# Splitting the final norm by token halves and moving late weight splits in a one-core streaming-encoder kernel

## Chip, cores and metric

The kernel runs on one NeuronCore of a Trainium2 chip. The metric is the device time of one execution in microseconds (us), lower is better; the time of before is the median of three runs. A profile gives every engine's instructions of one such execution, with times from the start of its span. The engines are TensorE (PE, matrix products; PEld is its weight load), VectorE (DVE), ScalarE (ACT), GpSimd (POOL), and SyncE (SP), which only issues transfers here.

## What is computed

One step of a one-layer encoder, for 512 prompt tokens and 32 sample tokens (544 together). A norm and a wide input projection feed two recurrent branches (an mLSTM with four heads, and HGRN2), which are merged by gates. The change lies in what follows the merge, at the end of the layer:

```python
y = jax.nn.sigmoid(ga) * ya + jax.nn.sigmoid(gb) * yb
h = h + y @ w_out[l]
h = h + jax.nn.sigmoid(h @ w_pg[l]) * (p[l] @ w_ple[l])
...
out = _rmsnorm(h, final_g)
```

`w_out` and `w_pg` are 1024 x 1024, `w_ple` is 256 x 1024. The mLSTM also returns its matrix memory C per head (512 x 512, with the normaliser as a further column), a product of all its keys and values; for the last head that product is computed at the very end of the kernel, between the steps of the final norm.

## The kernel before

**Layout.** Activations are kept transposed: 1024 channels as eight tiles of 128 partitions, with the 544 tokens as columns. A token half is 272 columns (`one`, `other`; `TH` = 272). float32 accuracy comes from splitting each operand into a high and a low part of a shorter format and adding three products (high x high, high x low, low x high). The high part is a cast on ScalarE (L132 for weights), the low part a subtraction (L133), on VectorE unless `eng` says otherwise.

**The wide products** `y @ w_out` and `h @ w_pg` use a two-by-two scheme with seven block products in place of eight. Class `Two` does this for a pair of output tiles, k and k+4: its weight blocks are a11, a12, a22 and sums s1 to s4, its moving operands are halves of the activation (`h1s`) or sums of those halves (`hf`, made by `half_sums`, L1995 to L2010, called by `h_sums`). Each block is twelve products of 128 x 272 on TensorE, accumulated in two PSUM tiles `d`, one for each token half. The methods `after1` to `after7` copy a partial sum to SBUF (`keep`, ScalarE, L609) or combine one with a PSUM tile into the output (`put`, VectorE L616 and L618, or ScalarE L620). An output tile pair has four quarters: tile 0 or 1, token half 0 or 1. `Pump` orders the blocks of four pairs, loads their weights three blocks ahead, and splits them. Trace names carry unit numbers: `wa11104` is block a11 of the first gate pair, `ws2107` is block s2 of the last. Split weights live in five rotating buffers, so a cast waits until TensorE has read the block five splits before it.

**Around the change**, in program order:

- the four pairs of `w_out`, whose `out` (L2057) adds the residual, splits the new h into high and low (L2062, L2063), and calls `h_sums` for the last pair (L2065);
- `ple_units(3, ...)` (L1979), the last three of eight embedding products `p @ w_ple` (names wple5 to wple7; twelve products of 128 x 272 each), their PSUM tiles copied out by L1987;
- the four pairs of `w_pg`. `gate_out` (L2089) applies the sigmoid, multiplies by the embedding product (L2093), adds to h (L2094), squares (L2095) and adds the square to a running sum `total` (L2097);
- the C memory of the last head (`memories`): three blocks of 24 products (L1041) and one of 2 x 12 (L1064), written out by ScalarE's queue. After five steps of six products `rms_cols` (L225 on) sums `total` over channels with tiny products into `r1pc` (L233) and takes the reciprocal root on VectorE with three Newton rounds (`rsqrt`, L183 to L185); after four more steps `norm_bcast` spreads the root over partitions with products `r1pb` (L248), and `norm_out` scales eight tiles of h (VectorE L2135, GpSimd L2132) and sends each as one transfer of y (SP, L2136).

**Order.** TensorE's order is the program's order (`manual_schedule`). The order on the other engines is set by the framework's scheduler when the program is built, from the data dependences and from marks such as `high_priority` and `issue_after`. Each engine works through its own list in order; an instruction that waits holds up all behind it.

Of the kernel before, what the change touches and what calls it, by code (L numbers as in the profile page):

```python
# [59 lines left out]
TAIL = (5, 4)  # L60
# [7 lines left out]
def hybrid_step(ctx: ExitStack, tc: tile.TileContext, a, o):  # L68
# [408 lines left out]
    class Two:  # L477
# [4 lines left out]
        def __init__(self, outs, early=False, apart=False, src=None, made_=None):  # L482
# [3 lines left out]
            self.hook = None  # L486
# [125 lines left out]
        def put(self, i, b, ps, t, how):  # L612
            with tc.high_priority(FIRST) if self.urgent else tc.high_priority():
                for d, c in self.tiles[i][1][b]:
# [4 lines left out]
                    else:  # L619
                        S.mul(d, ps[:, c], -1.0)  # L620

# [1435 lines left out]
    def out(f, t):  # L2057
# [6 lines left out]
        if f % HK == HK - 1 and h1[HK - 1] is not None and h1[KD - 1] is not None:  # L2064
            h_sums(HK - 1)  # L2065
# [20 lines left out]
    tokens = [(0, NS)] + [(NS + b * P, P) for b in range(NB)]  # L2086
    total = []

    def gate_out(f, t):  # L2089

        for c in (one, other) if f % HK == HK - 1 else (slice(0, T),):
            S.activation(t[:, c], t[:, c], AF.Sigmoid)
            V.tensor_tensor(t[:, c], t[:, c], ple[f][:, c], ALU.mult)  # L2093
            V.tensor_tensor(h1[f][:, c], h1[f][:, c], t[:, c], ALU.add)  # L2094
            S.activation(t[:, c], h1[f][:, c], AF.Square)  # L2095
            if total:
                V.tensor_tensor(total[0][:, c], total[0][:, c], t[:, c], ALU.add)  # L2097
        if not total:
# [8 lines left out]
            ("w_pg", k),  # L2107
        )
# [16 lines left out]
    def norm_out(pb):  # L2125
        rows = slot("rows")
        S.copy(rows[:, NS:T], pb[:, 0, :])
        S.copy(rows[:, :NS], pb[:, 1, :NS])  # L2128
        for f in (0, 4, 1, 2, 5, 3, 7, 6):
            t = h1[f]  # L2130
            if f in aside:
                G.tensor_tensor(t[:, :T], t[:, :T], rows[:, :T], ALU.mult)  # L2132
            else:
                for d, c in ((t[:, NS:T], pb[:, 0, :]), (t[:, :NS], pb[:, 1, :NS])):
# [125 lines left out]
```

## Time and profile before

| what | us |
|---|---|
| median of three runs | 1110.12 (1109.43 to 1111.32) |
| the profiled execution's own time | 1109.81 |
| its span in the profile | 1108.1 |
| TensorE busy with products | 1093.3 |
| VectorE busy | 924.2 |
| ScalarE busy | 693.0 |
| GpSimd busy | 206.2 |

Rows of the timeline read: start, duration (both us), engine, line, operation, output <- input, shape, and in square brackets how long the engine stood idle before it and what ended that. "x2" is two instructions merged into a row. Rows of one engine can overlap a little, since an instruction's start and its predecessor's end are pipelined. In a list of waits a row gives who waited for whom, the total, how often, and the longest.

### The profile page before, as it was taken

Reading aid. Unit: us, or ns where it says so; the run is one execution under the profiler, and the core shown is the slowest. Engines: PE = TensorE matmul, PEld = TensorE weight load, DVE = VectorE, ACT = ScalarE, POOL = GpSimd, SP = SyncE. Lnnn points to the kernel's source line nnn. Section 1 sums busy time; section 2 is a strip of 40 time slices with the busy share of each in tenths; the row PEclk is TensorE's granted clock in tenths of the full one; section 3 lists DMA queues with packets and bytes.
Section 4 is the critical chain, followed back from the end, with each engine's and each line's share of the span. In section 5 each row is a group of like instructions: output and inputs, shape, how many; then the busy total and the mean of one; then the engine's idle time right before and its main releaser. Section 6 shows DMA issues by size and latency. Waiting matters only on the chain. (4 is left out here: it accounts for less than half of the span.)

```text
span 1108.1 us, 23728 instructions
## 1 busy us (share of the span) xinstructions
PE 1093.3 (99%) x8621; PEld 1071.8 (97%) x8621; DVE 924.2 (83%) x2088; ACT 693.0 (63%) x1578; POOL 206.2 (19%) x370
## 2 busy tenths in 40 slices
PE   9999999999999999999999999999999999999897
PEld 9899999999999999999999999999999999999897
DVE  7889988686896786976888799999999977778785
ACT  6767557754666555665665477777676667446573
POOL 7204010303022031202220132232222210000001
PEclk9999999999999999999999999999999999999999
DMA  6135315639355286543898665666666682336843
GB/s 231 58 118 191 126 58 178 157 130 219 118 178 189 86 180 178 159 166 136 219 260 253 176 141 143 144 140 138 157 153 145 160 218 86 115 122 216 279 131 120
DMA packets 96398, 176.58 MB, mean 159 GB/s; under 512 B 11156, under 2 KB 16788, under 8 KB 96024
## 3 DMA queue, kind: packets, MB, share of 16 engines
q1 hardware_dynamic: 80352, 141.43, 39.9%
q0 software_dynamic: 15040, 32.51, 16.0%
q8 instruction: 68, 1.11, 0.4%
q10 hardware_dynamic: 888, 1.12, 0.3%
q14 instruction: 50, 0.41, 0.1%
HBM read 150.10 MB, written 41.69 MB: 173 GB/s over the span
## 5 line engine op out<-in xcount | busy, mean ns | idle before, releaser
L495 POOL DMA_DIRECT2D ws<-in_w_in x46 | 39.7, 862 | 211.0 <-DVE hkq L1818 35.6
L609 ACT COPY t<-d 128x272 f32<-128x272 f32 x153 | 58.1, 380 | 10.8 <-PE d L595 10.8
L1818 DVE TENSOR_TENSOR hkq<-hkq,q 128x288 f32<-128x288 f32 (+1 forms) x96 | 40.8, 432 | 2.8 <-PE pl L1800 1.1
L749 DVE SCALAR_TENSOR_TENSOR cv<-ub,vec,cv 128x547 f32<-128x547 f32 x48 | 37.6, 784 | 1.6 <-ACT cv L744 1.2
L2132 POOL TENSOR_TENSOR h<-h,rows 128x544 f32<-128x544 f32 x3 | 4.0, 1359 | 184.8 <-ACT rows L2128 184.8
L1800 PE MATMUL pl<-hkq,km 128*128 128x128 f32 x224 | 36.3, 283 | 1.0 <-ACT km L1786 1.0
L1786 ACT COPY km<-hkq 128x256 f32<-128x256 f32 x56 | 24.0, 428 | 14.6 <-DVE hkq L1818 5.9
L1800 PEld LDWEIGHTS pl<-hkq,km 128*128 128x128 f32 x224 | 30.3, 189 | 2.4 <-ACT km L1786 1.9
L1155 DVE SCALAR_TENSOR_TENSOR c<-c,wi,Cs 128x258 f32<-128x258 f32 x32 | 15.3, 479 | 18.6 <-PE Cs L1153 18.4
L1318 DVE TENSOR_TENSOR y<-ya,y 128x272 f32<-128x272 f32 x48 | 18.9, 435 | 12.0 <-PE ya L167 10.2
L1053 ACT COPY Co<-C 128x258 f32<-128x258 f32 x30 | 9.8, 378 | 29.6 <-PE C L1041 27.2
L1825 DVE COPY_PREDICATED at<-lmask,pl 128x256 f32<-128x256 uint8 (+1 forms) x56 | 25.3, 452 | 0.1
L741 POOL COPY uo<-ub 128x3 f32<-128x3 f32 x16 | 18.7, 1166 | 34.5 <-DVE ub L618 26.6
L1232 ACT COPY y<-nm 128x516 f32<-128x516 f32 x16 | 9.5, 591 | 22.9 <-PE nm L1221 22.4
L925 POOL COPY vsm<-vt 128x96 f32<-128x96 f32 x12 | 6.2, 517 | 86.1 <-ACT vt L620 43.8
L925 POOL COPY ksm<-kf 128x96 f32<-128x96 f32 x16 | 6.3, 399 | 84.3 <-ACT kf L939 84.3
L1765 POOL TENSOR_SCALAR_AFFINE_SELECT aa<-at 128x128 f32<-128x128 f32 x32 | 19.6, 643 | 8.2 <-DVE at L1825 8.0
L1209 DVE BATCH_NORM_STATS2 bs<-y 128x6 f32<-128x512 f32 (+1 forms) x20 | 13.8, 692 | 8.2 <-ACT y L1232 8.0
L570 POOL DMA_DIRECT2D ws<-in_w_in x14 | 14.1, 1007 | 32.3 <-DVE ws272l L133 26.8
L1221 PE MATMUL nm<-vhl,sh 128*128 128x258 f32 x112 | 18.4, 286 | 0.0
L376 POOL DMA_DIRECT2D w_pg_d<-in_w_pg x16 | 13.1, 816 | 24.0 <-issue 23.1
L1924 ACT ACTIVATE osq<-kq 128x128 f32<-128x128 f32 x32 | 9.8, 305 | 12.4 <-DVE kq L1919 12.1
(4733 smaller groups left out, 5083.8 us busy)
## 6 DMA issues: line engine op xcount, KB each, us to landing
ws<-in_w_in POOLq DMA_DIRECT2D x60, 256.0 KB, 4.8
ws<-in_w_in SPq DMA_DIRECT2D x46, 256.0 KB, 3.7
ya_d<-y SPq DMA_DIRECT2D x32, 272.0 KB, 2.5
y<-ya_d SPq DMA_DIRECT2D x24, 272.0 KB, 3.5
w_out_d<-in_w_out POOLq DMA_DIRECT2D x24, 256.0 KB, 6.0
w_pg_d<-in_w_pg POOLq DMA_DIRECT2D x24, 256.0 KB, 6.3
c<-in_C SPq DMA_DIRECT2D x16, 258.0 KB, 3.8
out_Cs<-c SPq DMA_DIRECT2D x16, 258.0 KB, 3.9
```

The lines of the kernel that those rows point to most:

```text
L495: G.dma_start(t, piece(u, i), accum_op=ALU.add)
L609: self.kept = S.copy(t, ps)
L741: G.tensor_copy(uo[:, ft, 0, :], ub[:, 547:550])
L749: V.scalar_tensor_tensor(cv[:, :547], ub[:, j : j + 547], vcol(V_CW + 4 * ft + j), cv[:, :547], ALU.mult, ALU.add)
L1155: V.scalar_tensor_tensor(c0[f][:, v], c0[f][:, v], wi[:, NS - 1 : NS], pn[:, :VH], ALU.mult, ALU.add)
L1221: PE.matmul(pn[:, g, :VH], st[j][x][:, (i - j) * P : (i - j + 1) * P], vv[j][y][:, g * VH : (g + 1) * VH], start=(j == 0 and q == 0), stop ...
L1318: add = V.tensor_tensor(y[:, half(b)], acc[b], y[:, half(b)], ALU.add)
L1765: G.affine_select(out=out, in_=x, compare_op=ALU.is_gt, fill=0.0, base=0, pattern=[[-sign, n]], channel_multiplier=sign)
L1786: low = S.copy(km.rearrange("p (n j c) -> p n j c", j=2, c=c), view(kk, HB, ((2 * c, NA // (2 * c)), (c - HB, 2), (1, c))),)
L1800: PE.matmul(out, km[:, b * P : (b + 1) * P], view(qq, b * P, dims), start=True, stop=True)
L1818: V.tensor_tensor(x, x, d, ALU.mult)
L1825: V.copy_predicated(at[:, :n], lmask[:, li, :n], pn[:, 0, :n])
```

## The change

It has three parts.

1. The low splits of wple5 to wple7 go from VectorE to GpSimd, and the sums of h for the last pair are made after the first two gate weights are split, not in `out`.
2. The last gate pair gets its own block order (`parts`): a11, a12, s2, a22, s3, s1, s4. It uses four PSUM tiles, and `gate_out` runs for each quarter as it is complete: tile 0 and tile 1 of the first token half, then tile 1 and tile 0 of the second.
3. The final norm runs for each token half by itself: column sums, root, broadcast, scaling, and eight transfers of y of 128 x 272 for each half. The first half's column sums stand after one step of C, the second half's after five, followed at once by the first half's broadcast; the second half's broadcast comes four steps later.

```diff
-TAIL = (5, 4)
+TAIL = (4, 4)
...
         def blocks(self, times):
+            if self.parts:
+                m, (s2, s1, s3, a22, s4) = self.made, sorted(times[2:])
+                return [
+                    (times[0], [(a, 0)], self.make("a11"), self.run("a11", 0, True, self.after1), []),
+                    (times[1], [(a, 1)], self.make("a12"), self.run("a12", 1, True, self.first), []),
+                    (s2, [(m, 1)], self.make("s2"), self.run("s2", 0, False, self.after6), []),
+                    (s1, [(b, 1)], self.make("a22"), self.run("a22", 2, True, self.second), []),
+                    (s3, [(m, 2)], self.make("s3"), self.run("s3", 0, False, self.third), []),
+                    (a22, [(m, 0)], self.make("s1"), self.run("s1", 1, True, self.fourth), [k[1]]),
+                    (s4, [(m, 3)], self.make("s4"), self.run("s4", 3, True, self.fifth), [k[0]]),
+                ]
...
+                if half == 2:
+                    self.ps = self.ps + phalves(f"d{self.other}")
...
+        def done(self, i, b, ps, t, how):
+            self.put(i, b, ps, t, how)
+            self.parts(i, b, self.tiles[i][0])
+
+        def first(self, ps):
+            self.done(0, 0, ps, self.t["t1"], "add")
+
+        def second(self, ps):
+            self.keep("t4", ps)
+
+        def third(self, ps):
+            self.keep("t167", ps)
+            self.done(1, 0, ps, self.t["t4"], "minus")
+
+        def fourth(self, ps):
+            t = self.t["t16"]
+            with tc.high_priority():
+                V.tensor_tensor(t, t, ps, ALU.add)
+            self.done(1, 1, ps, self.t["t167"], "minus")
+
+        def fifth(self, ps):
+            self.done(0, 1, ps, self.t["t16"], "add")
...
-                w = weight(a["w_ple"][f], f"wple{f}", cols=2 * P)
+                w = weight(a["w_ple"][f], f"wple{f}", cols=2 * P, eng=V if f < 5 else G)
...
-        if f % HK == HK - 1 and h1[HK - 1] is not None and h1[KD - 1] is not None:
-            h_sums(HK - 1)
...
-    tokens = [(0, NS)] + [(NS + b * P, P) for b in range(NB)]
+    blocks = ((0, P), (P, P), (2 * P, TH - 2 * P))
...
-    def gate_out(f, t):
+    def gate_out(f, t, c=slice(0, T)):
...
+            (lambda i, b, t: gate_out(HK - 1 + i * HK, t, half(b))) if k == HK - 1 else None,
...
-    def norm_bcast(r):
-        pb = paux("r1pb")
-        for b in range(NB):
-            bcast(pb[:, 0, b * P : (b + 1) * P], r, b + 1, P)
-        bcast(pb[:, 1, :NS], r, 0, NS)
+    def norm_bcast(b, r):
+        pb = paux(f"r1pb{b}")
+        for i, (t0, m) in enumerate(blocks):
+            bcast(pb[:, 0, t0 : t0 + m], r, i, m)
         return pb
...
-    def norm_out(pb):
-        rows = slot("rows")
-        S.copy(rows[:, NS:T], pb[:, 0, :])
-        S.copy(rows[:, :NS], pb[:, 1, :NS])
+    def norm_out(b, pb):
+        rows = slot(f"rows{b}")
+        S.copy(rows[:, :TH], pb[:, 0, :TH])
         for f in (0, 4, 1, 2, 5, 3, 7, 6):
-            t = h1[f]
+            t = h1[f][:, half(b)]
             if f in aside:
-                G.tensor_tensor(t[:, :T], t[:, :T], rows[:, :T], ALU.mult)
+                G.tensor_tensor(t, t, rows[:, :TH], ALU.mult)
             else:
-                for d, c in ((t[:, NS:T], pb[:, 0, :]), (t[:, :NS], pb[:, 1, :NS])):
-                    V.scalar_tensor_tensor(d, d, vcol(V_FG + f), c, ALU.mult, ALU.mult)
-            nc.sync.dma_start(o["y"][f], t[:, :T])
+                V.scalar_tensor_tensor(t, t, vcol(V_FG + f), pb[:, 0, :TH], ALU.mult, ALU.mult)
+            nc.sync.dma_start(o["y"][f, :, half(b)], t)
...
         pump = Pump(gates_)
+        pump.prepare(2)
+        h_sums(HK - 1)
         pump.to(2)
...
         rest = memories()
+        next(rest)
+        r = rms_cols(total[0][:, one], blocks, "r10")
+        norm_scale()
         for _ in range(TAIL[0]):
             next(rest)
-        r = rms_cols(total[0], tokens, "r1")
-        norm_scale()
+        r1 = rms_cols(total[0][:, other], blocks, "r11")
+        norm_out(0, norm_bcast(0, r))
         for _ in range(TAIL[1]):
             next(rest)
-        norm_out(norm_bcast(r))
+        norm_out(1, norm_bcast(1, r1))
```

VectorE's list at the head of the gate product, before: `h3u`, `h3v`, `hfl`, `hfx` are the sums of h for the last pair and their low parts, the names with `l` behind a number are low splits of weights.

```order
L2058 TENSOR_TENSOR h_14848<-h_14848,res_14846 128x544
L1998 TENSOR_TENSOR h3u<-h_14845 128x272
L1999 TENSOR_TENSOR h3u<-h_14848,h_14845 128x272
L2000 TENSOR_TENSOR h3v_15029<-h3u,h_14848 128x272
L2063 TENSOR_TENSOR h_15005<-h_14845,h_15005 128x272
L2001 TENSOR_TENSOR h3v_15030<-h3v_15029,h_14848 128x272
L2063 TENSOR_TENSOR h_15022<-h_14848,h_15022 128x544
L2007 TENSOR_TENSOR hfl_15026<-h3u,hfh_15025 128x544
L2008 TENSOR_TENSOR h_15005<-h3v_15030,h_15005 128x272
L2009 SCALAR_TENSOR_TENSOR hfx_15027<-h3v_15029,hfx_15027 128x272
L133 TENSOR_TENSOR wple60l<-wple6r_15064,wple60h 128x256
L133 TENSOR_TENSOR wple70l<-wple7r_15087,wple70h 128x256
```

The same place on VectorE now, from the low part of the new h on:

```order
L2099 TENSOR_TENSOR h_15005<-h_14845,h_15005 128x272
L133 TENSOR_TENSOR wa11104l<-wi104r_15097,wa11104h 128x512
L133 TENSOR_TENSOR wa12104l<-wi104r_15099,wa12104h 128x512
L2099 TENSOR_TENSOR h_15022<-h_14848,h_15022 128x544
L2034 TENSOR_TENSOR h3u<-h_14845 128x272
L2035 TENSOR_TENSOR h3u<-h_14848,h_14845 128x272
L2036 TENSOR_TENSOR h3v_15121<-h3u,h_14848 128x272
L133 TENSOR_TENSOR ws2104l<-ww_pg0r_15101,ws2104h 128x512
L2037 TENSOR_TENSOR h3v_15122<-h3v_15121,h_14848 128x272
L133 TENSOR_TENSOR ws1104l<-ww_pg0r_15103,ws1104h 128x512
L2044 TENSOR_TENSOR h_15005<-h3v_15122,h_15005 128x272
L2043 TENSOR_TENSOR hfl_15118<-h3u,hfh_15117 128x544
```

The embedding splits have left VectorE's list, and four weight splits that stood behind the sums now stand among or ahead of them; `hfx` of the last pair is the next row behind those shown. GpSimd's list gains three rows ahead of the norm's:

```order
L133 TENSOR_TENSOR wple50l<-wple5r_15025,wple50h 128x256
L133 TENSOR_TENSOR wple60l<-wple6r_15048,wple60h 128x256
L133 TENSOR_TENSOR wple70l<-wple7r_15071,wple70h 128x256
L2164 TENSOR_TENSOR h_14404<-h_14404,rows_15832 128x272
L2164 TENSOR_TENSOR h_14510<-h_14510,rows_15832 128x272
```

Before, GpSimd's list had nothing between its last transfers and the norm's three products. The third place is the end of VectorE's list. Before, the running sum `pg_15148` is finished, then one chain of the root follows:

```order
L2094 TENSOR_TENSOR h_14848<-h_14848,pg_15565 128x272
L2097 TENSOR_TENSOR pg_15148<-pg_15148,pg_15565 128x272 x2
L240 TENSOR_SCALAR rms_s<-r1pc 32x1
L240 TENSOR_SCALAR rms_s<-r1pc 128x4
L180 TENSOR_SCALAR rsq_t<-rms_s 128x5
L181 TENSOR_SCALAR rms_r<-rsq_t 128x5
```

Now two chains run into each other; this piece is the end of the first half's root (`r10pc`) and the beginning of the second's (`r11pc`):

```order
L185 SCALAR_TENSOR_TENSOR rms_r<-rsq_u,rms_r 128x3
L240 TENSOR_SCALAR rms_s<-r11pc 128x2
L183 TENSOR_TENSOR rsq_u<-rms_r 128x3
L240 TENSOR_SCALAR rms_s<-r11pc 16x1
L184 SCALAR_TENSOR_TENSOR rsq_u<-rsq_u,rms_s 128x3
L180 TENSOR_SCALAR rsq_t<-rms_s 128x3
L185 SCALAR_TENSOR_TENSOR rms_r<-rsq_u,rms_r 128x3
L181 TENSOR_SCALAR rms_r<-rsq_t 128x3
```

The last Newton round of the first half (L183, L184, and the second L185 row) now stands behind the reading of `r11pc`, which TensorE makes four steps of C later than `r10pc`; likewise the reading of `r10pc` stands ahead of the last quarter's addition to h.

More of the change, by code (lines that the diff above doesn't have):

```diff
@@ L2085, in hybrid_step @@
     kw, vv = xs[:NB], xs[NB:]
-    tokens = [(0, NS)] + [(NS + b * P, P) for b in range(NB)]
+    blocks = ((0, P), (P, P), (2 * P, TH - 2 * P))
     total = []
-    def gate_out(f, t):
[L2091 to L2098, printed above, removed]
+    def gate_out(f, t, c=slice(0, T)):
+        S.activation(t[:, c], t[:, c], AF.Sigmoid)
+        V.tensor_tensor(t[:, c], t[:, c], ple[f][:, c], ALU.mult)
+        V.tensor_tensor(h1[f][:, c], h1[f][:, c], t[:, c], ALU.add)
+        S.activation(t[:, c], h1[f][:, c], AF.Square)
+        if total:
+            V.tensor_tensor(total[0][:, c], total[0][:, c], t[:, c], ALU.add)
+        else:
             total.append(t)
```

4 lines of the change are left out of this document (2 added, 2 removed).

## Prediction

> **What bounds the kernel now.** I start with the page, then ask who made TensorE wait, since that engine is busy 99% of the span.
>
> ```profile
> span 1108.1 us, 23728 instructions
> PE 1093.3 (99%) x8621; PEld 1071.8 (97%) x8621; DVE 924.2 (83%) x2088; ACT 693.0 (63%) x1578; POOL 206.2 (19%) x370
> ```
>
> The view of TensorE's waits over the whole span has one long entry (the next is 1.1 us), and it lies just where the change works:
>
> ```profile
> PE ple L167 <- DVE wple60l L133: 4.2, 1, 4.2
> ```
>
> The chain of waits that ended last shows what it holds up, and that everything behind it is TensorE's own work up to the last eviction:
>
> ```profile
> 1040.00 0.35 DVE wple60l L133
> ...
> 1040.39 4.30 PE ple L167 x20
> 1044.69 42.08 PE d L595 x336
> 1086.77 3.63 PE C L1041 x30
> 1090.40 1.14 PE r1pc L233 x10
> 1091.54 2.99 PE C L1041 x24
> 1094.53 1.22 PE r1pb L248 x10
> ...
> 1101.02 0.37 ACT Co L1071
> ```
>
> So a microsecond taken from TensorE before 1086 is a microsecond of the span. Behind 1101.4 only transfers are left; they are the second bound, weighed below.
>
> **The embedding products and the last sums of h.** TensorE's rows around the wait, two products to a row, and then four stage windows (width, then busy time of TensorE, its weight loads, VectorE, ScalarE and GpSimd, granted clock, DMA share, GB/s):
>
> ```profile
> 1034.05 0.41 PE L167 MATMUL ple<-ps0h,wple50h 128*128 128x272 f32 x2
> 1035.56 0.41 PE L167 MATMUL ple<-ps0h,wple60h 128*128 128x272 f32 x2
> 1040.39 0.56 PE L167 MATMUL ple<-ps0h,wple60l 128*128 128x272 f32 x2 [4.18 <-DVE wple60l L133]
> 1044.53 0.41 PE L595 MATMUL d<-h,wa11104h 128*128 128x272 f32 x2
> 1035.80:1040.39 4.59, 0.41 (x5) 0.20 (x3) 4.59 (x12) 3.00 (x8) 0.00 (x0) 1.00 0.99 334
> 1040.39:1042.30 1.91, 1.91 (x9) 1.91 (x10) 1.91 (x4) 0.41 (x1) 0.00 (x0) 0.59 0.97 321
> 1042.30:1044.30 2.00, 2.00 (x12) 2.00 (x11) 0.87 (x2) 0.78 (x3) 0.00 (x0) 0.54 0.80 213
> 1044.30:1046.00 1.70, 1.70 (x16) 1.70 (x15) 0.69 (x1) 1.20 (x3) 0.00 (x0) 1.00 0.91 295
> ```
>
> Six rows took 1.51 us before the wait (1034.05 to 1035.56), 0.252 each. After it ten rows took 4.14 (1040.39 to 1044.53), 0.414 each: the granted clock is 0.59 and 0.54 in those two windows and 1.00 in the next. The wait thus costs twice: 4.33 us of delay (1040.39 less 1036.06, two rows after 1035.56, when it was due), and 10 x 0.162 = 1.62 us of slow products. Without it the first product of wa11104 starts at 1035.56 + 12 x 0.252 = 1038.57 in place of 1044.53: **5.96 us** is the most this edit can give.
>
> What is late next? These rows give the prices of what now stands in another order:
>
> ```profile
> 1032.87 0.43 DVE L616 TENSOR_TENSOR h<-d,t 128x272 f32<-128x272 f32 x1
> 1033.03 0.39 ACT L132 CAST wple70h<-wple7r 128x256 fp32r<-128x256 f32 x1
> 1034.90 1.36 DVE L2058 TENSOR_TENSOR h<-h,res 128x544 f32<-128x544 f32 x2
> 1039.55 0.44 DVE L2009 SCALAR_TENSOR_TENSOR hfx<-h3v,hfx 128x272 fp32r<-128x272 f32 x1
> 1039.91 0.42 DVE L133 TENSOR_TENSOR wple60l<-wple6r,wple60h 128x256 fp32r<-128x256 f32 x1
> 1040.58 0.69 DVE L133 TENSOR_TENSOR wa11104l<-wi104r,wa11104h 128x512 fp32r<-128x512 f32 x1
> ```
>
> A row overlaps the next by some 0.08 us (1039.55 to 1039.91 is 0.36 for a row of 0.44), so start to start an operation of 272 columns takes 0.35 us, one of 512 takes 0.60, one of 544 takes 0.64, and a low split of an embedding weight 0.35. The first two gate blocks need wa11104l and wa12104l, which now stand ahead of the sums; the third, s2, needs hfx of the last pair in its tenth product, 34 products after 1038.57. At 42.08 / 336 = 0.125 us each that is 1042.8. On VectorE the residual adds begin at 1034.55 (1034.90 less the 0.35 of wple50l, which is gone). From there the new order holds two adds (1.27), seven operations of 272 columns (2.45), four low splits of 512 (2.40) and two of 544 (1.28): hfx is done at 1041.95, near 1042.25 with a ScalarE cast or two waited for. That is in time by 0.6 us, so nothing would be late.
>
> But three splits of 256 columns now run on GpSimd while VectorE is full, and the trace shows at its start what that can do:
>
> ```profile
> 11.62 1.98 DVE L1382 SCALAR_TENSOR_TENSOR x<-x,x 128x544 fp32r<-128x544 f32 x1
> 14.00 0.77 DVE L1382 SCALAR_TENSOR_TENSOR x<-x,x 128x544 fp32r<-128x544 f32 x1
> 11.67 1.35 POOL L1395 TENSOR_TENSOR r0q<-r0q,r0q 128x544 f32<-128x544 f32 x1
> 1096.55 4.00 POOL L2132 TENSOR_TENSOR h<-h,rows 128x544 f32<-128x544 f32 x3 [184.78 <-ACT rows L2128]
> ```
>
> VectorE's operation at 11.62 took 1.98 us where its twin took 0.77: it stood still for about as long as GpSimd's product ran. From 4.00 / 3 = 1.33 us for 544 columns, a split of 256 takes about 0.63 on GpSimd. Three make 1.9 us in which VectorE may stand; some of it falls beside an operation that reads PSUM (the row at 1032.87). I take 1.4 us, with 0 and 1.9 as ends. Then hfx comes at 1043.65, 0.8 us late, and the gain of this part is 5.96 - 0.8 = **5.15 us** (4.6 to 5.96). GpSimd itself is in time: the last of its high parts is cast by 1033.4 (one operation later in the new order), so even one after the other behind a VectorE operation each, the three lows end near 1033.6, 1034.8 and 1035.7, and are due at 1034.55, 1036.05 and 1037.6.
>
> The Trainium skill, "SBUF — State Buffer", section "Who interferes with whom", says that a VectorE instruction with two inputs in SBUF contends with a GpSimd instruction that reads SBUF, as an exclusive lock. The rows at 11.62 and 11.67 agree. By that rule alone all 1.9 us would fall on VectorE and this part would give 4.6; without it, 5.96.
>
> Moved with it, at no cost: on SP's queue fourteen loads of the kept keys and values now stand behind two gate weights that wait for GpSimd's splits. They are first used at 1086, forty microseconds later. From the second gate pair on VectorE's order is nearly the old one.
>
> **The last gate pair and the norm.** The last pair has the same 84 products in another order and takes two more PSUM tiles; the first C block then reuses tiles whose last reader is VectorE's put of the quarter before the last, about 0.5 us ahead. I cost that at nothing. The norm's path is what changes:
>
> ```profile
> 1084.56 0.43 DVE L618 SCALAR_TENSOR_TENSOR pg<-t,t 128x272 f32<-128x272 f32 x1
> 1088.89 1.02 DVE L2097 TENSOR_TENSOR pg<-pg,pg 128x272 f32<-128x272 f32 x2
> 1091.58 0.22 DVE L240 TENSOR_SCALAR rms_s<-r1pc 32x1 f32<-32x1 f32 x2 [1.66 <-PE r1pc L233]
> 1093.84 0.17 DVE L185 SCALAR_TENSOR_TENSOR rms_r<-rsq_u,rms_r 128x5 f32<-128x5 f32 x1
> ```
>
> In the clock of before: TensorE reaches the first half's column sums (r10pc) after six C products, 1086.77 + 6 x 0.121 = 1087.5. VectorE gets the put of that half done from 1084.56 on; behind it stand seven operations at 0.35 with two short waits (for the next block's end, and for a square from ScalarE), so total's first half is complete near 1088.0. **First new wait, 0.5 us** (0 to 1). Now VectorE: the order places the reading of r11pc ahead of the last Newton round of the first half's root. r1pb0 on TensorE comes directly behind r11pc, so it waits until VectorE has read r11pc and run three dependent operations of 0.20 (the row distance between 1091.58 and 1093.84 is 2.26 for eleven): **second new wait, 0.9 us** (0.6 to 1.4). Before, 24 products lay between r1pc and r1pb as cover (2.99 us); that cover is gone for the first half. The small products grow from 20 to 24: 4 x 0.118 = 0.5. TensorE's end moves out by 0.5 + 0.9 + 0.5 = 1.9 us against the block before it.
>
> What that costs at the end depends on the transfers:
>
> ```profile
> 1103.40 0.78 SPq L2136 DMA_DIRECT2D out_y<-h  x1
> 1105.00:1106.00 1.00, 0.00 (x0) 0.00 (x0) 0.00 (x0) 0.00 (x0) 0.00 (x0) 0.79 0.97 377
> 1106.00:1107.00 1.00, 0.00 (x0) 0.00 (x0) 0.00 (x0) 0.00 (x0) 0.00 (x0) 0.50 0.04 15
> 1101.43 0.34 ACTq L1072 DMA_DIRECT2D out_Cp<-Co  x1
> out_Cp<-Co ACTq DMA_DIRECT2D x1, 258.0 KB, 2.5
> ```
>
> The eight y transfers keep the DMA engines full at 377 GB/s until 1106, 5 us after TensorE's last product (the chain's 1101.02). With the change y goes out in two sets of eight; the eight more issues cost SP 0.34 us each, the least that an issue takes here, beside the waiting for data. r1pb0 starts at 1088.0 + 0.7 + 2.9 (24 C products) + 0.7 + 0.9 = 1093.2, 1.3 us before r1pb did, and each half then takes half the time. So y stops being last, and C's last half is: issued at 1101.43 + 1.9 = 1103.3, landing at most 2.5 us later (the last row: the undisturbed one at 1090.27, of twice the size; I take 2.2) at 1105.5, against 1106.1 now. The tail gains **0.6 us**; with no new waits 2.1, with them at twice the size -0.8.
>
> **Sum.** 5.15 + 0.6 = 5.75 us off the profiled execution's own time of 1109.81 (its span of 1108.1 and 1.7 around it): **1104.0 us**. That execution lies 0.3 us below the median of the three runs, 1110.12, inside their 1109.43 to 1111.32.
>
> **Rivals.** *VectorE doesn't feel GpSimd*: the splits fall beside PSUM reads or the 0.6 us of room absorbs them. 5.96 + 0.6, or up to 2.1 in the tail: 1102 to 1103.3. Against it the row at 11.62; for it that not every VectorE operation will meet one of GpSimd's. *The tail loses*: the halved norm does not bring y out earlier in effect, as both new waits stand at their upper ends or r1pb1 waits too, because the second half's root runs beside GpSimd's products. 5.15 - 0.8 and worse: 1105.3 to 1107. For it: VectorE's order interleaves both roots. *The wait only moves*: the last sums, now behind four weight splits, come 3 us or more behind s2, and the tail gives nothing: 1107 to 1110. Against it: the count of operations above, which would have to be 40% off. *Slower*: VectorE has no gap (4.59 busy of 4.59 in the first window) until it lacks ws1104h, near 1040.5 in the new order (that cast needs the buffer of wple60, which TensorE would still hold). If GpSimd's splits got their turn only in such a gap, wple50l would be ready near 1041.2, 6.6 us late, with slow products after it: 16 rows x 0.252 + 1.6 put wa11104 at 1046.9, 2.3 later than now, and a poor tail 0.8 more: 1112 to 1113. It decides once wple50l ends after 1039. Against it: GpSimd's product at 11.67 took its turn at once in spite of a running VectorE operation.
>
> The Trainium skill, "TensorE: Matmul & The Clock Gate", section "What's actually happening", lets the clock fall after an idle window of about 3.4 us. The 4.18 us wait and the 0.59 behind it agree; by it the new waits of 0.5 and 0.9 cost only their length, and a clock that fell there too would take about the 1.6 us more that it took here, 1105.6, which lies inside the second rival.
>
> **Chances.** Forecast 0.45; no lock 0.15; the tail loses 0.25; the wait only moves 0.11; slower 0.04. The first three hold 0.85, from 1102 to 1107, so the range is 1102.0 to 1107.2. About 0.2% (2.2 us) is what a measurement of this kernel can tell from no change. Faster by more: the first three and half of the fourth, 0.90; within it 0.06; slower 0.04.
>
> **What would show it.** TensorE's waits lose wple60l, and ple, then wa11104, run at a granted clock of 1.00; if not, the first part is wrong. A wait of 0 to 1.3 us at hfx in s2, and VectorE operations of 1 us or more beside wple50l to wple70l, show the lock. Two waits, at r10pc and r1pb, of 0.5 and 0.9 show the tail; the last transfer should be C's, not y's. The prediction is wrong if gate products wait for any weight split later on, or if y is still the last to land.

## The result, and the profile after

The changed kernel takes 1106.38 us (median of eight runs, 1103.89 to 1107.32), the kernel before 1110.06 beside it. The ratio is 0.9962, with a 95% interval of 0.9949 to 0.9975: 4.2 us faster (2.8 to 5.7). The forecast of 1104.0 was 2.4 us too low. The page's first lines barely differ from those of before:

```profile
span 1104.8 us, 23775 instructions
PE 1093.3 (99%) x8625; PEld 1070.3 (97%) x8625; DVE 925.5 (84%) x2101; ACT 692.7 (63%) x1577; POOL 210.6 (19%) x376
```

A single span holds chance as well. What the change does is seen when both executions are cut at the same instructions (starts of rows on TensorE; us):

| stretch | before | after | forecast |
|---|---|---|---|
| start to the first product with wple50 | 1034.05 | 1035.29 | no change |
| from there to the first product with wa11104 | 10.48 | 5.20 | 4.52 |
| from there to the first product of C | 42.08 | 42.27 | 42.88 |
| from there to the end of the span | 21.49 | 22.08 | 20.9 |

The first row is not the change's: it arises in the first 200 us (TensorE busy 196.6 us there, 198.0 before), and in the twelve further profiles this point lies between 1033.7 and 1036.0. One of them, of a kernel that leaves the embeddings as they were, has 1035.35. The second and third rows are part one: 5.1 us gained, where 5.15 was forecast. The fourth is the tail: 0.59 lost, where 0.6 gain was forecast.

**The head.** The list of TensorE's waits from 1030 to 1100 no longer has wple60l; it holds only the two forecast for the norm:

```profile
PE r1pb L248 <- DVE rms_r L181: 0.8, 1, 0.8
PE r10pc L233 <- DVE pg L2130: 0.6, 1, 0.6
```

TensorE's timeline at the embeddings, two products to a row, and one stage window over it (width; busy TensorE, weight loads, VectorE, ScalarE, GpSimd; granted clock, DMA share, GB/s):

```profile
1035.29 0.41 PE L167 MATMUL ple<-ps0h,wple50h 128*128 128x272 f32 x2
...
1036.80 0.59 PE L167 MATMUL ple<-ps0h,wple60h 128*128 128x272 f32 x2
1037.23 0.41 PE L167 MATMUL ple<-ps0l,wple60h 128*128 128x272 f32 x2
...
1038.24 0.41 PE L167 MATMUL ple<-ps1h,wple60l 128*128 128x272 f32 x2
1038.71 0.68 PE L167 MATMUL ple<-ps0h,wple70h 128*128 128x272 f32 x2
1039.23 0.41 PE L167 MATMUL ple<-ps0l,wple70h 128*128 128x272 f32 x2
...
1040.49 0.28 PE L608 MATMUL d<-h,wa11104h 128*128 128x272 f32 x1
```
```profile
1035.29:1040.49 5.20, 5.14 (x39) 4.68 (x37) 5.20 (x9) 4.20 (x13) 1.10 (x2) 1.00 0.87 270
```

The clock is 1.00, as forecast. Eighteen rows at 0.252 would take 4.53; three steps that are longer than that (0.43, 0.47 and 0.52) make up the other 0.67. Why is seen on the timelines of GpSimd, VectorE and ScalarE:

```profile
1033.82 0.74 POOL L133 TENSOR_TENSOR wple50l<-wple5r,wple50h 128x256 fp32r<-128x256 f32 x1 [119.99 <-ACT wple50h L132]
1034.52 0.93 POOL L133 TENSOR_TENSOR wple60l<-wple6r,wple60h 128x256 fp32r<-128x256 f32 x1
1035.69 0.94 POOL L133 TENSOR_TENSOR wple70l<-wple7r,wple70h 128x256 fp32r<-128x256 f32 x1 [0.24 <-ACT wple70h L132]
```
```profile
1033.87 0.98 DVE L2037 TENSOR_TENSOR h2v<-h2v,h 128x272 f32<-128x272 f32 x1
1034.78 0.43 DVE L629 TENSOR_TENSOR h<-d,t 128x272 f32<-128x272 f32 x1
1035.13 0.91 DVE L2043 TENSOR_TENSOR hfl<-h2u,hfh 128x544 fp32r<-128x544 f32 x1
1035.96 0.98 DVE L2044 TENSOR_TENSOR h<-h2v,h 128x272 fp32r<-128x272 f32 x1
...
1044.27 0.43 DVE L2045 SCALAR_TENSOR_TENSOR hfx<-h3v,hfx 128x272 fp32r<-128x272 f32 x1
```
```profile
1037.95 0.42 ACT L2098 CAST h<-h 128x272 fp32r<-128x272 f32 x1 [1.00 <-DVE h L2094]
1038.28 0.67 ACT L2023 COPY pleo<-ple 128x272 f32<-128x272 f32 x2
```

Each split on GpSimd meets one VectorE operation with both inputs in SBUF, and that one takes 0.91 to 0.98 us; the one that reads PSUM (d, at 1034.78) takes its usual 0.43 although a split runs beside it. ScalarE then stands 1.00 us for VectorE's residual add, and copies the embedding product out behind that; the products with wple70, which need the PSUM tiles, start late. (That the late copies are the reason is read from the order of these rows. In e3_sums below, where nothing runs on GpSimd, the first copy starts 2.03 us behind the first product with wple50, here 2.99, and all these steps are 0.25 but the two around its one wait.) So the price of GpSimd is paid here, and not at hfx: the last one ends at 1044.70, and TensorE reads it without a wait.

**The tail.** TensorE from the first product of C on; both waits are in the places forecast, and r1pb1 waits for nothing:

```profile
1082.76 0.40 PE L1077 MATMUL C<-xh,xh 128*128 128x258 f32 x2
...
1084.27 0.71 PE L233 MATMUL r10pc<-ones,pg 128*128 128x2 f32 x6 [0.63 <-DVE pg L2130]
...
1089.34 1.00 PE L248 MATMUL r1pb<-ident,rms_r 128*128 128x128 f32 x6 [0.80 <-DVE rms_r L181]
...
1093.26 0.99 PE L248 MATMUL r1pb<-ident,rms_r 128*128 128x128 f32 x6
```

r1pb0 starts 6.58 us behind the first product of C; 6.6 were forecast. But y has not become early: its last data ends 20.32 us behind the first product of C, 0.29 later than before, and C's last half ends 0.22 behind that. SP's timeline as a whole, and the one issue of it that starts at 1095.60; then ScalarE's copies and issues of C's last tile:

```profile
1091.64 9.47 SPq L2167 DMA_DIRECT2D out_y<-h  x16
```
```profile
1095.60 1.92 SPq L2167 DMA_DIRECT2D out_y<-h  x1
```
```profile
1098.08 0.38 ACT L1107 COPY Co<-C 128x258 f32<-128x258 f32 x1 [0.90 <-PE C L1100]
1099.40 0.34 ACTq L1108 DMA_DIRECT2D out_Cp<-Co  x1
1099.78 0.37 ACT L1107 COPY Co<-C 128x258 f32<-128x258 f32 x1 [1.33 <-PE C L1100]
1101.19 0.34 ACTq L1108 DMA_DIRECT2D out_Cp<-Co  x1
```

And the stage windows by single microseconds (the last two numbers are the DMA engines' share and their GB/s):

```profile
1095.00:1096.00 1.00, 1.00 (x11) 1.00 (x10) 1.00 (x4) 0.00 (x0) 1.00 (x2) 1.00 1.11 362
1096.00:1097.00 1.00, 1.00 (x11) 1.00 (x10) 0.83 (x3) 0.48 (x2) 0.99 (x2) 1.00 0.59 202
1097.00:1098.00 1.00, 1.00 (x11) 1.00 (x9) 0.00 (x0) 0.17 (x1) 0.00 (x0) 1.00 0.06 13
1098.00:1099.00 1.00, 1.00 (x11) 1.00 (x10) 0.00 (x0) 0.38 (x1) 0.00 (x0) 1.00 1.00 361
...
1102.00:1103.00 1.00, 0.00 (x0) 0.00 (x0) 0.00 (x0) 0.00 (x0) 0.00 (x0) 1.00 0.68 227
```

Three things are new. The ninth issue of y, the first of the second half, holds SP for 1.92 us, and the DMA engines run dry for some 1.4 us. C's last two issues come 0.94 and 1.04 us after their copies. And the engines move 361 GB/s where they moved 377 with whole rows: a packet of 1088 bytes takes 48 ns in the trace, one of 2176 bytes 88 (medians).

The order of ScalarE's instructions with their waits names the cause of the second. A transfer of SP or ScalarE signals its end on one of eight semaphores, in turn; the next one on the same semaphore waits for it. Before, one of the last three issues of C had such a wait, after it all three have:

```
L1090 DMA out_Cp<-Co_15920 128x516 [waits DMAHW7_49,Activation_49]
L1107 COPY Co_15926<-C_15924 128x258 [waits PE_49]
L1108 DMA out_Cp<-Co_15926 128x258 [waits DMAHW3_49,Activation_49]
L1107 COPY Co_15926<-C_15925 128x258 [waits PE_49]
L1108 DMA out_Cp<-Co_15926 128x258 [waits DMAHW6_49,Activation_49]
```

### The profile page after: what moved, and what is told of

Its sections match the earlier page's. It is cut to its first block, busy times and chain, and to the rows that moved or that the text cites. A ratio compares the mean times of both kernels' runs of the same rounds, so it can differ in the third digit from the quotient of the medians.

```text
span 1104.8 us, 23775 instructions
## 1 busy us (share of the span) xinstructions
PE 1093.3 (99%) x8625; PEld 1070.3 (97%) x8625; DVE 925.5 (84%) x2101; ACT 692.7 (63%) x1577; POOL 210.6 (19%) x376
## 4 chain that ended last, share of the span: by engine, by line
PE 90%; DVE 5%; DMA 3%; issue 1%; ACT 1%; SPq 0%; POOL 0%; ACTq 0%; DVEq 0%
PE d L608 43%; PE ya L167 9%; PE yb L167 4%; PE k L167 4%; PE q L167 4%; PE C L1077 3%; PE nm L1257 3%; PE pl L1836 2%; PE vp L1580 2%; PE u L291 2%; PE d L460 2%; PE sc L1037 2%; DMA ws<-in_w_in 1%; PE ple L167 1%; PE kt L1122 1%
```

## Experiments

Twelve kernels ran, each beside the kernel before. Ratios are to before, with their 95% intervals; 0.001 is 1.1 us. Since an interval is some 2.8 us wide, what is said of less than that goes by stretches cut as above, from each kernel's profile.

**The parts by themselves.** First, the head's edits alone on the kernel before (line numbers of `out`, `ple_units` and the main program):

```diff
-w = weight(a["w_ple"][f], f"wple{f}", cols=2 * P)
+w = weight(a["w_ple"][f], f"wple{f}", cols=2 * P, eng=V if f < 5 else G)
-        if f % HK == HK - 1 and h1[HK - 1] is not None and h1[KD - 1] is not None:
-            h_sums(HK - 1)
         pump = Pump(gates_)
+        pump.prepare(2)
+        h_sums(HK - 1)
         pump.to(2)
```

> The kernel before with the first part of the change alone: the last three low splits of the embeddings on GpSimd, and the last sums of h behind the first two gate weights. The last pair and the norm stay as before. Theory (from the traces: this part takes 5.1 us off TensorE's path, the tail then gives 0.5 back, and the 1.2 us by which the changed kernel's profile reached this place later arose in its first 200 us and is chance): 5.1 us faster than before, so about 0.7 to 1 us faster than the whole change. Rival 1 (the forecast's: the tail gains 0.6, so this part must be smaller than it looks): 3.5 to 4 us faster, a little slower than the whole change. Rival 2 (the 1.2 us of the first 200 us belongs to the change): 3.9 us faster, and the same 1.2 us shows in this run's first 200 us.

Measured: 1104.89 us, ratio 0.9952 (0.9940 to 0.9964), 5.3 us faster. From wple50 to the first product of C it takes 47.49 us, 5.07 less than before; the tail is 21.43, as before (21.49). Its wple50 comes at 1035.35, but so does that of the next kernel, which does not touch the head, so the 1.2 us are chance. The theory holds.

Second, the changed kernel with those same lines undone, so that only the last pair's order and the halved norm are left:

> The kernel before with the second part of the change alone: the last pair's order by halves of the tokens and the norm by halves, 16 transfers of y in place of 8. Embeddings' splits and the sums of h stay as before, so TensorE's wait for wple60l of some 4.2 us stays. Theory (the tail loses): 0.3 to 0.8 us slower than before, two TensorE waits at r10pc and r1pb of 0.6 and 0.8, y still landing at the very end beside C. Rival (the forecast): 0.6 us faster, C's last half alone at the end.

Measured: 1111.87 us, ratio 1.0013 (1.0004 to 1.0021), 1.4 us slower. TensorE's three long waits in the profile:

```profile
PE ple L167 <- DVE wple60l L133: 4.2, 1, 4.2
PE r1pb L248 <- DVE rms_r L181: 0.8, 1, 0.8
PE r10pc L233 <- DVE pg L2132: 0.6, 1, 0.6
```

From the first product of C to the end it takes 22.23 us, 0.74 more than before, and from wple50 to the first product of C 52.55, as before (52.56). So the loss stands in the tail. The last pair's order and the halved norm together lose, by themselves and beside part one; this is the forecast's wrong sign. The 0.74 lies in the theory's 0.3 to 0.8; the measured 1.4 is above it, but its interval reaches down to 0.4. The last pair's order without the halved norm was not run.

Third and fourth, the two halves of the head's edit, one without the other:

```diff
 third, e3_sums: as the first, but without GpSimd
+w = weight(a["w_ple"][f], f"wple{f}", cols=2 * P)
 fourth, e4_pool: only this line changed against before
+w = weight(a["w_ple"][f], f"wple{f}", cols=2 * P, eng=V if f < 5 else G)
```

> The first part of the change without GpSimd: the last sums of h behind the first two gate weights, but all low splits stay on VectorE. Theory (moving the sums suffices; three splits of 0.35 us on VectorE cost it 1.05, about what the lock beside GpSimd costs it, 1.27): wple60l is ready 0.5 us late, no other wait; 5.0 to 5.4 us faster than before, the same as with GpSimd within 0.5. Rival (the GpSimd splits carry the gain): wple60l still holds TensorE for 2 us or more with a slower clock behind it, 1 to 3 us faster than before.

> The other half of the first part alone: the last three low splits of the embeddings on GpSimd, the last sums of h at their old place. Theory: wple60l and wple70l come in time from GpSimd, the sums are then ahead of wa12104l on VectorE, which is ready about 1 us late; 4 to 5 us faster than before, a little less than both together. Rival (only moving the sums helps; the wait moves from wple60l to the first gate weights): 1 to 2 us faster, with a TensorE wait of 3 us or more for wa11104l or wa12104l. Lock on VectorE as in the whole change: operations of 0.9 us or more beside wple50l to wple70l, GpSimd's splits at 0.7 to 0.95 us.

The moved sums alone: 1104.93 us, ratio 0.9948 (0.9935 to 0.9960), 47.58 us from wple50 to C. GpSimd alone: 1105.91, ratio 0.9962 (0.9949 to 0.9975), 48.69 us. Of the third's waits in the region there is one, of the fourth's two:

```profile
1037.32 0.52 PE L167 MATMUL ple<-ps0h,wple60l 128*128 128x272 f32 x2 [0.44 <-DVE wple60l L133]
```
```profile
1040.05 0.39 PE L595 MATMUL d<-h,wa11104l 128*128 128x272 f32 x1 [0.37 <-DVE wa11104l L133]
1042.35 0.39 PE L595 MATMUL d<-h,wa12104l 128*128 128x272 f32 x1 [0.53 <-DVE wa12104l L133]
```

Either edit gains most of the 5.07 us that both gain in this stretch: 4.98 with the sums, 3.87 with GpSimd. Beside the moved sums GpSimd is worth 0.09 us in this pair of profiles, which is less than they scatter. The stretch took 47.46 to 48.67 us, 47.93 on average, in the seven profiles with both edits at the head (the changed kernel, e1_head, and below e5, e6, e10, e11 and e12), and 47.26 to 47.58, 47.41 on average, in the four with the sums alone (e3_sums, and below e8, e9 and e13). In four of the seven (e5, e10, e11, e12) TensorE waits 0.2 to 0.7 us at block s4 of the first gate pair, since ScalarE's cast of its weight stood until the weight's transfer had landed; in e10_gq:

```profile
ACT ws4104h L132 <- DMA ww_pg0r<-w_pg_d: 2.4, 1, 2.4
```

In none of the four with the sums alone does TensorE wait there. Why that transfer lands late no run shows. VectorE's timeline of e3_sums shows the lock's price, since the same operations run there with nothing on GpSimd:

```profile
1033.88 0.43 DVE L2001 TENSOR_TENSOR h2v<-h2v,h 128x272 f32<-128x272 f32 x1
1034.23 0.72 DVE L2007 TENSOR_TENSOR hfl<-h2u,hfh 128x544 fp32r<-128x544 f32 x1
...
1035.22 0.43 DVE L2008 TENSOR_TENSOR h<-h2v,h 128x272 fp32r<-128x272 f32 x1
```

Against these rows (0.43, 0.72, 0.43) the changed kernel's 0.98, 0.91 and 0.98 are 1.29 us more: GpSimd takes three splits of 0.35 (1.05 us) off VectorE and costs it 1.29.

**Why the tail loses.** The next eight change the tail of the changed kernel. All are level with it in time, as their intervals go, so here is each one's tail in its profile. Times are us from the first product of C; "last data" is the end of the last packet with data of y and of C in the trace, and the span ends 1.3 to 1.7 us behind the later of the two.

| kernel | ratio to before | TensorE's end | first y issue | y's last data | C's last data | end of span |
|---|---|---|---|---|---|---|
| before | 1 | 14.38 | 11.33 | 20.03 | 17.89 | 21.49 |
| changed | 0.9962 | 16.72 | 8.89 | 20.32 | 20.54 | 22.08 |
| e5_queue | 0.9960 | 16.73 | 8.90 | 19.43 | 20.59 | 21.93 |
| e6_order | 0.9969 | 19.04 | 8.02 | 19.48 | 21.19 | 22.60 |
| e8_both | 0.9962 | 17.56 | 8.02 | 20.28 | 20.67 | 22.17 |
| e9_all | 0.9963 | 17.57 | 8.03 | 19.72 | 20.50 | 22.01 |
| e10_gq | 0.9958 | 16.74 | 8.90 | 20.04 | 20.48 | 22.18 |
| e11_cover | 0.9962 | 15.29 | 8.96 | 20.06 | 18.86 | 21.60 |
| e12_cover_gq | 0.9958 | 15.29 | 8.95 | 19.79 | 20.18 | 21.89 |
| e13_two_issuers | 0.9957 | 15.31 | 8.98 | 20.12 | 20.20 | 21.76 |

The first four of these moved three transfers to another queue, or put TensorE's small products in another order, or both:

```diff
 e5_queue
-nc.sync.dma_start(o["y"][f, :, half(b)], t)
+(nc.scalar if b and f in (1, 5, 7) else nc.sync).dma_start(o["y"][f, :, half(b)], t)
 e6_order
-next(rest)
+for _ in range(2): next(rest)
 r = rms_cols(total[0][:, one], blocks, "r10")
 for _ in range(TAIL[0]): next(rest)
+pb = norm_bcast(0, r)
 r1 = rms_cols(total[0][:, other], blocks, "r11")
-norm_out(0, norm_bcast(0, r))
+norm_out(0, pb)
 e8_both: e6_order, and all low splits on VectorE
 e9_all: e8_both, and the line of e5_queue
```

> The changed kernel, with three of the second half's eight y transfers issued from ScalarE's queue in place of SP's (row tiles 5, 1 and 7). In the profile of the changed kernel the ninth issue of y on SP takes 1.92 us and the DMA engines stand almost idle for 1.4 us beside it. Theory (y and C's last half end together, within 0.2 us, since TensorE's two new waits of 0.6 and 0.8 put C's end out; so relieving SP alone gives next to nothing): same as the changed kernel within 0.5 us, about 4 us faster than before. Rival (SP's issues are what bounds the end): 1.2 us or more faster than the changed kernel, 5.3 us faster than before.

> The changed kernel with TensorE's small products of the norm in another order: the first half's column sums after two steps of C in place of one, and the broadcast of the first half's root directly ahead of the second half's column sums, not behind them, so that VectorE ends the first root without reading r11pc first. Theory (the two new waits of TensorE are what the halved norm costs): both waits go, TensorE ends 1.2 to 1.4 us earlier, y's second half comes 1 us earlier, 0.9 to 1.4 us faster than the changed kernel, about 5.2 us faster than before. Rival (the transfers or SP's long issue bound the end): TensorE's waits go and the time stays within 0.4 us of the changed kernel.

> The new order of the norm's small products as in the run before this, with the first part cut down to the moved sums of h (all low splits on VectorE). Theory (the parts add up: moved sums alone 5.8 off, halved norm 1.4 on, its two waits 1.2 off): 5.4 to 5.8 us faster than before, level with the moved sums alone. Rival (without its waits the halved norm gains what the forecast hoped, up to 2 us): 7 us or more faster than before.

> As the run before this one, and three y transfers of the second half on ScalarE's queue. Theory (with TensorE's waits gone y alone is late, by SP's long ninth issue, so now relieving SP shows): 0.5 to 1.2 us faster than the run before this one, 6.2 us or more faster than before. Rival (the issue is long because the transfers ahead of it are not done, whatever queue it comes from): level with the run before this one within 0.4 us.

*e5_queue* came out at the time of its theory, the changed kernel's: y ends 0.9 us earlier and C no earlier. But it does not test SP alone, since the edit delays C in another way: ScalarE, which also copies and issues C, stands for GpSimd's tile and for older transfers, and issues C's last half 19.23 us behind the first product of C, where it was 18.43:

```profile
ACT Co L1089 <- POOL h L2164: 2.9, 1, 2.9
ACT Co L1107 <- DMA out_y<-h: 2.5, 1, 2.5
```

*e6_order* did not do as its theory said. The two waits did not go; TensorE's timeline has them in new places and sizes:

```profile
1088.68 1.00 PE L248 MATMUL r1pb<-ident,rms_r 128*128 128x128 f32 x6 [0.41 <-DVE rms_r L185]
...
1094.99 1.00 PE L248 MATMUL r1pb<-ident,rms_r 128*128 128x128 f32 x6 [1.54 <-DVE rms_r L185]
```

The second root now stands between the first half's products on VectorE, beside GpSimd's, and ends later. (Of e6's late end, 19.04, a lower granted clock in that one profile is a part: 0.91 from 1083 to 1103, against 1.00 in e8, the same tail.) So this pair said nothing on what the waits cost. *e8* and *e9* show the parts adding up no better than before: 4.2 and 4.1 us faster than before by their ratios, where 5.4 to 5.8 and 6.2 or more were expected. In e9 relieving SP again moved y (19.72) and hardly C (20.50); it is level with e8, as its rival said, which does not show the rival's reason.

The next three gave both roots cover on TensorE, or moved three transfers to GpSimd's queue, whose semaphores are others, or both:

```diff
 e11_cover: steps of C ahead of r10pc, r11pc, r1pb0 and r1pb1
-1, 4, 0, 4
+2, 3, 2, 3
 e10_gq
+(nc.gpsimd if b and f in aside else nc.sync).dma_start(o["y"][f, :, half(b)], t)
 e12_cover_gq: both
```

> The changed kernel, with the second half's three y transfers of GpSimd's tiles (4, 5, 6) issued from GpSimd's own queue. That queue has completion semaphores of its own, so the eight that SP's and ScalarE's transfers share in turn are free earlier; in the changed kernel's profile the two issues of C's last tile stood 0.94 and 1.03 us behind their copies, each waiting for an older transfer on its semaphore. Theory (C's end is late by TensorE's waits and by these semaphores, y's end by SP's issues; lifting both the semaphores and SP's load moves both ends): C's last issues follow their copies by under 0.5 us, last data of y and of C 0.5 to 1 us earlier, 0.5 to 1.0 us faster than the changed kernel, 4.7 to 5.2 us faster than before. Rival (TensorE's end alone decides): the same as the changed kernel within 0.3. Rival (GpSimd's issues of some 0.9 us each come too late): 0.5 us or more slower than the changed kernel.

> The changed kernel with cover for both roots on TensorE: two steps of C ahead of the first column sums, three ahead of the second, two ahead of the first broadcast, three ahead of the second. VectorE then ends both roots ahead of the first products with them. In the run with the other order TensorE's two waits of 0.6 and 0.8 had only given way to two of 0.4 and 1.6, since the second root stood between the first half's products on VectorE; here there should be none. Theory (y's end, by SP's issues, and C's end, by TensorE and the shared semaphores, lie within 0.2 us of each other, so one alone gives little): TensorE without a wait in the tail, its end 1.2 to 1.4 us earlier against the first product of C, and the time 0 to 0.6 us below the changed kernel, 4.2 to 4.8 us faster than before. Rival (TensorE's waits are the whole loss of the tail): 1.2 us or more faster than the changed kernel, 5.4 us or more faster than before.

> The two edits of this call together: cover on TensorE for both roots, and three y transfers of the second half on GpSimd's queue. Theory (each end is moved by its own edit): both ends 1.2 us or more earlier against the first product of C, 1.2 to 1.8 us faster than the changed kernel, 5.4 to 6 us faster than before, so that the halved norm is worth 0 to 0.6 us. Rival (transfers of half a row are slower by themselves, 355 GB/s in the changed kernel against 377 in the one before, and that bounds the end): within 0.5 us of the better of the two edits alone.

In *e11_cover* TensorE has no wait in the tail, as the timeline shows (no brackets):

```profile
1084.53 0.71 PE L233 MATMUL r10pc<-ones,pg 128*128 128x2 f32 x6
...
1089.67 1.00 PE L248 MATMUL r1pb<-ident,rms_r 128*128 128x128 f32 x6
...
1092.87 0.93 PE L248 MATMUL r1pb<-ident,rms_r 128*128 128x128 f32 x6
```

TensorE ends 1.43 us earlier, C's last data 1.68 earlier, and y's only 0.26: the span ends 0.48 earlier, in the 0 to 0.6 of the theory. The waits were not the whole loss. In *e10_gq* C's last issues follow their copies by 0.42 and 0.03 us, so the semaphore waits are gone, and C's last issue comes 1.25 us earlier; yet its last data comes at 20.48, 0.06 earlier. It waits in the DMA engines, which move 344 to 366 GB/s from 16 to 19 us behind the first product of C. The theory that the shared semaphores held C's end falls. *e12_cover_gq* is no better than e11 (21.89 against 21.60), which is what its rival said.

The last run put two transfers of the first half on ScalarE's queue, where ScalarE is idle, on top of e11 and the moved sums:

```diff
+(nc.scalar if b == 0 and f in (2, 3) else nc.sync).dma_start(o["y"][f, :, half(b)], t)
```

> The run with cover for both roots, and two y transfers of the first half (row tiles 2 and 3) issued from ScalarE's queue, which is idle at that time; the head with the moved sums alone (all low splits on VectorE). In the run with cover C's last data ends 18.9 us behind the first product of C, y's 20.1, and SP issues 16 transfers one behind the other, some 0.5 us each however small, from 9.0 to 18.4. Theory (with TensorE's waits gone SP's sixteen issues are what sets y's end): SP's last issue and y's last data come 0.8 to 1 us earlier (19.1 to 19.3), the span ends 20.7 to 21.0 behind the first product of C, against 22.1 in the changed kernel and 21.4 to 21.5 with the norm of before; 5.8 to 6.3 us faster than before, level with or a little better than the moved sums alone. Rival (the data of half rows bound it): y's last data stays at 19.8 to 20.2 and the span at 21.6.

SP's last issue comes 0.4 us earlier than in e11, half of what the theory asked for, and y's last data not at all (20.12), as the rival said. By its ratio the kernel is 4.8 us faster than before, where 5.8 to 6.3 were expected. So the theory that sixteen issues one behind the other set y's end gets no support. The run is not a clean test of it either: ScalarE now waits 3.1 us for transfers of y ahead of its last two copies, so C is as late as y:

```profile
ACT Co L1107 <- DMA out_y<-h: 3.1, 2, 2.0
```

The best versions are those that leave the norm whole: e1_head and e3_sums, with ratios of 0.9952 and 0.9948 against 0.9962 of the changed kernel. Their intervals overlap with that of the changed kernel; that the new tail by itself is slower is what e2_tail shows.

## Why the prediction was partly right

**What bounds the kernel**: right. The wait for wple60l is gone, and the time with it.

**Part one**: right in its sum (5.15 forecast, 5.1 measured in the stretches, 5.3 by e1_head), and in its two main terms: the wait and the slow clock behind it both went, and GpSimd cost VectorE 1.29 us where 1.4 was taken. The step behind that was wrong in its place. hfx was not 0.8 us late but in time; the 0.67 lost stand in the embedding products, which waited for ScalarE's copies behind a late VectorE. The two errors nearly cancelled, by luck: the first gate product came 0.67 later than forecast, which gave hfx as much more time. The Trainium skill, "SBUF — State Buffer", section "Who interferes with whom", has a VectorE instruction with two inputs in SBUF contend with a GpSimd instruction that reads SBUF, and one with at most one such input, outside the modes that use two ports, not; the 0.43 of the operation that reads PSUM beside a split agrees, and so do the 0.91 to 0.98 of the other three. That GpSimd was not needed could have been read from the forecast's own prices (three splits of 0.35 saved, 1.4 paid), but it was e3_sums that showed it: either edit alone takes away most of the wait. Of the forecast's signs, the VectorE operations beside the splits came at 0.91 to 0.98 us, just under the 1 us that it named. That no gate product waits for a weight split holds in this profile, and not in four of the other six with the same head; so the step "Moved with it, at no cost", on SP's loads, has no support from them.

**The tail**: the wrong step is the one that put its parts together, "each half then takes half the time. So y stops being last". The forecast had C's last half land at 1105.5, which is 18.9 in the table's time, and y ahead of it. In fact y ended at 20.32 and C at 20.54; in e2_tail y was the last again (20.65 and 20.44). The terms ahead of it were good: waits of 0.63 and 0.80 (0.5 and 0.9 forecast), r1pb0 at 6.58 (6.6). TensorE's end moved out by 2.34 (1.9 forecast): the four more small products and the seams to them cost some 0.9 in place of 0.5. But the forecast worked out when the first half's y starts, and never when the second's ends. y's first issue is 2.44 us earlier, its last issue 1.2 later (18.03, before 16.80) and its last data 0.29 later, so 2.7 us are lost between. A reckoning by the rows of the changed kernel, which no run with one thing changed confirms: 1.4 us in which the engines run dry behind the long ninth issue; 0.7 for the tile of C (258 KB at 361 GB/s) that now runs inside y's stretch and ran ahead of it before; 0.3 for the slower half rows (2.23 MB at 361 and at 377 GB/s); and a slow first microsecond (0.09 MB). And C's last half was given an issue at 16.7 and 2.2 us to landing on empty engines; it had a semaphore to wait for, was issued at 18.43, and met full ones. The second rival, "the tail loses", had the sign and a price of 0.8; 0.59 is what the stretch shows, and the measured 1106.38 lies between its bounds. Three slips in the sums weigh little beside that: y's last data before ended at 1106.64, not at 1106.1; the tail without new waits would gain 0.6 + 1.4 = 2.0, not 2.1; and the second rival's times begin at 1109.81 - 4.35 = 1105.5, not at 1105.3.

**What stays open.** No single edit of the tail gave it back. With TensorE's waits gone, with the semaphore waits gone, with SP relieved, one of the two ends stayed at 20.0 to 20.6. The hole alone is not the price: in e5_queue the ninth issue takes 0.41 us and the engines move 361 and 330 GB/s in the two microseconds where the changed kernel's moved 283 and 7, and C still ends at 20.59, by ScalarE's late issue. In e10_gq most of it is filled (337 and 222 GB/s) and C's issues are not late, and C ends at 20.48. Nor does a limit by the bytes still to be moved fit, since the engines are not full at the very end. In e10_gq they move 29 and 19 GB/s in the half microseconds from 19.5 and from 20.0, with at most two packets of data at a time for the last 0.8 us. A packet of 1088 bytes in 48 ns is 23 GB/s, so that is one or two of the sixteen engines, ending behind the others. In the kernel before, too, the last 0.6 us has at most two packets at a time. Which engines these are, and why, no run shows.

## What to carry to other kernels

When a wait is removed by two edits at once, try each alone: here a move of a few sums in one engine's order gave nearly all of it, and beside it the offload to a second engine gave nothing that its lock did not take back. Splitting a result so that it leaves earlier helps only if the last piece leaves earlier: work out the end of the last piece, with its issues, its waits for shared semaphores and the other transfers in its stretch, not the start of the first. Cut two executions at common instructions before their spans are compared; here chance in the first 200 us hid a quarter of the gain between the two profiles.

## What the runs showed of the hardware

Long DMA issues on SP and ScalarE coincide with instruction fetches (a 16 KB packet on a queue of its own). The changed kernel's ninth y issue runs from 1095.60 to 1097.52; the fetch beside it runs from 1095.71 to 1097.14. The DMA view of the changed kernel from 1095.5 to 1098 has the fetch as the row of q8 (packets, MB, share of the engines); the row above gives the rate in forty slices:

```profile
GB/s 348 383 348 628 331 296 314 366 348 366 348 314 348 348 313 383 279 122 70 0 0 0 0 0 0 17 0 17 0 17 0 17 0 17 0 17 17 35 17 35
...
q1 hardware_dynamic: 407, 0.39, 46.1%
q8 instruction: 1, 0.02, 3.6%
```

No packet starts from 1096.73 to 1097.12; as the fetch's packet ends, packets of y follow one another one at a time up to 1097.95, as if one DMA engine's share of y had stood behind the fetch. In the fourteen profiles 123 issues of 0.8 us or more on SP and ScalarE overlap such a packet, and 114 of them end 0.31 to 0.42 us behind its end. It is no rule that an issue beside a fetch is held: 693 shorter ones overlapped one too, and 34 long ones had none, among them the fifth to seventh whole-row transfers of y (1.05 to 1.14 us each). This is a coincidence in time that was counted, not a cause that a run has shown.
